# Weight chunks two ahead in the last pair of a part, pinned additions, and another split of the next layer's dots

## The chip, the cores and the metric

The kernel runs on one core of one Trainium2 chip. The metric is the device time of one execution in microseconds; the median of several runs is compared. Five engines work side by side, each through its own instructions in order: TensorE (PE, with its weight loads PEld), VectorE (DVE), ScalarE (ACT), GpSimd (POOL) and SyncE (SP). In this kernel SP only starts transfers from memory; POOL starts those that add into their destination.

## What is computed

Two layers of a decoder trunk on x of 512 tokens by 1024 features. The half of a layer that matters here, cut from the reference:

```
mod = (c_act @ w_ada + b_ada)                      # c_act = silu(c), 1024 numbers
sh1, sc1, g1, sh2, sc2, g2 = jnp.split(mod, 6, axis=-1)
h = rmsnorm(x, norm1_w) * (1 + sc1) + sh1
...                                                # mixers, attention, gates
x = x + g1 * (merged @ w_out)
h2 = rmsnorm(x, norm2_w) * (1 + sc2) + sh2
x = x + g2 * ((jax.nn.silu(h2 @ w_gate) * (h2 @ w_up)) @ w_down)
```

`w_gate` and `w_up` are 1024 x 2816, `w_down` 2816 x 1024: 22 column blocks of 128. The next layer begins with the same norm of the new x, so it needs its own `sc1` and `sh1` by then, and `sc2` and `sh2` later.

## The kernel before

**Layout and numbers.** x lies transposed in on-chip memory, as eight tiles of 128 features by 512 tokens. Every float32 operand of a product is split into a high and a low part (`whi`/`wlo` for weights, two `big` tiles for activations), and a product is three matmuls (`mm3`, L158): high by high, high by low, low by high.

**Weights.** They come in chunks of up to eight 128 x 128 blocks, in the order of use. `next_w(ahead)` (L350) loads until more than `ahead` chunks are waiting (four by default) and hands out the oldest. Loading a chunk means: `fetch` starts its transfer on SP into one of three `raw` buffers, ScalarE copies the high part (`whi`, L326), VectorE subtracts for the low part (`wlo`, L329). There are five `whi` and five `wlo` buffers. The subtraction is pinned: it keeps its place in program order among VectorE's pinned instructions, where a scheduler places the others.

**The feed-forward part.** The 22 column blocks go in four parts, `PARTS` (L47): three blocks along the loop over k, one single and one pair; then three, two and three pairs. After its columns a part runs its down stage: for each of the eight output blocks n it sums over the part's nk = 6, 6, 4, 6 blocks into one PSUM bank, and VectorE adds the result to x (`residual`, L954). A pair (`glu_pair`, L1050) computes two column blocks of gate (z = 0) and up (z = 1) by Strassen-like forms. It uses seven chunks in four steps: B21 and B11; R1 and -V; B22 and T3; T4. TensorE accumulates a[z] over B11, -V, T3 and T4, and VectorE must read a[z] between T3 and T4: `V.tensor_add(m22, m22, a[z])`, L1081, once for each z. The products are then made on ScalarE (`Silu`) and VectorE (L1090, L1092, L1093) and split (`split_from`: high part on ScalarE L511, low part on VectorE L512). A last pair of a part has down chunks behind it; the other pairs have the chunks of the next pair.

**Sums.** Four of the seven chunks of a pair are sums of weight blocks. Per matrix, `Sums.begin` (L250) has POOL load two blocks into `w4` tiles (L255) and add two more on top by transfers (L257); `Sums.first` (L259) lets VectorE add the remaining ones (L263, L264). `w4` has six buffers. `begin` is called four chunks ahead of loading, so the first pair of a part has its sums loaded while the last pair of the part before runs, and the second pair's during the down stage.

**The dots.** `mod` of a layer comes without TensorE: for each of the six vectors and each of eight blocks j, `ada_step` (L397) loads 512 KB of `w_ada` by SP into a `w4` tile and VectorE multiplies it with `csil` and sums along the row (`ada_dot`, L375, one instruction and a short read of the accumulator). `ada_end` (L402) adds the bias and, for SC1 and SC2, folds the norm weight in. `ada_tasks` (L410) makes a list of nine tasks for each vector: eight dots at cost 1.2 and an end at 0.2. Such lists go into a queue `bulk`; each four products of TensorE are a tick, a tick adds `bulk_rate` to a credit, and tasks are issued while the credit isn't negative. The dots of layer 1 for its first norm (SC1, SH1) go to the down stages of parts 0 and 1 of layer 0, those for its second norm to part 2 (five tasks), to the tail of part 3 (four) and to layer 1's loop along k (the rest, at rate 0.6).

**The loop along k.** Layer 1 starts with a loop over the eight k blocks (first three of them in two halves of 256 tokens) that makes q and three feature blocks at once, while VectorE still makes the norm's later k blocks (L482, L485).

Of the kernel before, what the change touches and what calls it, by code (L numbers as in the profile page):

```python
# [46 lines left out]
PARTS = ((3, 1, 1), (0, 0, 3), (0, 0, 2), (0, 0, 3))  # L47

SUMS_AHEAD = 4
AHEAD2 = 5  # L50

RAW, BIG = 3, 46

# [25 lines left out]
def hybrid_trunk(ctx, tc, xT, ws, ada, cols, pool_w, qk_w, crow, pos, con, out):  # L79
# [72 lines left out]
    def pin(ins):  # L152
        return tc.keep_in_program_order(ins)
# [162 lines left out]
                items.append((None, (l, blocks)))  # L316
    at = [0, 0]
    loaded = deque()
    hold = [None]

    def rawt():
        return wp.tile([P, C_BLOCKS, P], F32, tag="raw", name=nm("raw"), bufs=RAW)
# [27 lines left out]
    def next_w(ahead=None):  # L350
        ahead = ahead_now[0] if ahead is None else ahead
        while at[0] < len(items) and len(loaded) <= ahead:
            loaded.append(load_w())
        return loaded.popleft()
# [18 lines left out]
    def ada_dot(aw, l, part, j):  # L373

        return V.scalar_tensor_tensor(aw, aw, 1.0, csil, op0=ALU.mult, op1=ALU.mult,  # L375
                                      accum_out=mod[l][:, part, j:j + 1])
# [20 lines left out]
    def ada_step(l, part, j, early):  # L397
        aw = wp.tile([P, D], F32, tag="raw", name=nm("raw"), bufs=RAW) if early else w4([P, D])
        nc.sync.dma_start(aw, ada[l, part, j])
        pin(ada_dot(aw, l, part, j))  # L400

    def ada_end(l, part):  # L402
        m = mod[l][:, part]
# [6 lines left out]
    def ada_tasks(l, parts, early=False):  # L410
        out = []
        for part in parts:
            for j in range(KT):
                out.append((1.2, lambda part=part, j=j: ada_step(l, part, j, early)))
            out.append((0.2, lambda part=part: ada_end(l, part)))
        return out
# [90 lines left out]
    def split_from(src, scale=None):  # L507

        hi, lo = bigt(), bigt()
        if scale is None:  # L510
            A.activation(hi, src, AF.Copy)  # L511
            V.tensor_sub(lo, src, f32(hi))  # L512
        else:
            A.activation(hi, src, AF.Copy, scale=scale)
            V.scalar_tensor_tensor(lo, src, scale, f32(hi), op0=ALU.mult, op1=ALU.subtract)  # L515
        return hi, lo
# [199 lines left out]
    for l in range(L):  # L716
# [7 lines left out]
        for n, (k, lo, hi) in enumerate([(k, 0, S) for k in range(KT)] if l == 0 else HALVES + REST):  # L724
            if l == 0:
                if k + 3 < KT:
                    first.append(ada_first_load(k + 3))
                if k + 2 < KT:
                    ada_first(k + 2, first[k + 2], SC1)
                    ada_first(k + 2, first[k + 2], SH1)  # L730
                    norm.first_scaled(k + 2)
                    norm.first_hi(k + 2)
                loaded.append(load_w())
                if k + 2 < KT:
                    norm.first_lo(k + 2)
            if k not in held:
                held[k] = next_w(0 if l == 0 else None)
            if l > 0 and n == 1:
                second(norm, l, 0, bank)
                bulk.extend(later)  # L740
                bulk_rate[0] = 0.6
            w = held[k]
            h = norm.k(k)
            for t in range(lo // P, hi // P):
                mm3(q_ps[t], cut(h, slice(None), slice(t * P, (t + 1) * P)), wrow(w, 0), k == 0, k == KT - 1)
            for z in range(3):
                mm3(f_ps[z][:, lo:hi], wblk(w, 4 + z), cut(h, slice(None), slice(lo, hi)),
                    k == 0 and lo == 0, k == KT - 1)
# [298 lines left out]
                mm3(o, wblk(w, 4 * g + c), forms[c][name], start and c == 0, c == HK - 1,  # L1047
                    skip_group_check=not start)

        def glu_pair():  # L1050

            both = range(2)
            e = [ps_pair()[:, 0, :BLOCK] for _ in both]
            a, c = [None] * 2, [None] * 2
            one, two = [None] * 2, [None] * 2
            w = [next_w() for _ in both]
            for z in both:
                group(e[z], w[z], 1, "B21", True)
            for z in both:
                a[z], one[z] = ps_mm()[:, :BLOCK], tmp()  # L1060
                group(a[z], w[z], 0, "B11", True)
                C11 = one[z][:, :BLOCK]
                A.activation(C11, a[z], AF.Copy)
                V.tensor_add(C11, C11, e[z])
            w = [next_w() for _ in both]
            for z in both:
                c[z], two[z] = ps_mm()[:, :BLOCK], tmp()
                group(c[z], w[z], 0, "R1", True)
                A.activation(two[z][:, BLOCK:], c[z], AF.Copy)
            for z in both:  # L1070
                group(a[z], w[z], 1, "-V", False)
                A.activation(one[z][:, BLOCK:], a[z], AF.Copy)
            w = [next_w() for _ in both]
            for z in both:
                group(c[z], w[z], 0, "B22", False)
                C12 = one[z][:, BLOCK:]
                V.tensor_add(C12, C12, c[z])
            for z in both:
                group(a[z], w[z], 1, "T3", False)
                m22 = two[z][:, BLOCK:]  # L1080
                V.tensor_add(m22, m22, a[z])  # L1081
            w = next_w()
            for z in both:
                group(a[z], w, z, "T4", False)

            (g1, u1), (g2, u2) = one, two
            A.activation(g1, g1, AF.Silu)
            A.activation(g2[:, BLOCK:], g2[:, BLOCK:], AF.Silu, scale=-1.0)
            A.activation(g2[:, :BLOCK], a[0], AF.Silu, scale=-1.0)
            V.tensor_mul(u1, u1, g1)  # L1090
            act.append(split_from(u1))
            V.scalar_tensor_tensor(u2[:, BLOCK:], u2[:, BLOCK:], -1.0, g2[:, BLOCK:], op0=ALU.mult, op1=ALU.mult)  # L1092
            V.scalar_tensor_tensor(u2[:, :BLOCK], a[1], -1.0, g2[:, :BLOCK], op0=ALU.mult, op1=ALU.mult)  # L1093
            act.append(split_from(u2))

        for part, (along, single, pairs) in enumerate(PARTS):
            act = []
            nk = along + single + 2 * pairs
            if along:
                held = {}  # L1100
                for n, (k, lo, hi) in enumerate(HALVES + REST):
                    if n == 1:
                        second(norm, l, 1, bank)
                        table(AF.Silu, norm.y[:, 0:1])
                    if k not in held:
                        held[k] = next_w()
                    for z in range(2 * FA):
                        mm3(f_ps[z][:, lo:hi], wblk(held[k], z), cut(norm.k(k), slice(None), slice(lo, hi)),
                            k == 0 and lo == 0, k == KT - 1)
                    if k >= HK:  # L1110
                        make_forms(k - HK)
                del held
                for z in range(FA):
                    glu(f_ps[z], f_ps[FA + z])
            for _ in range(single):
                wg = next_w()
                g = ps_mm()
                feature_tile(g, wg)
                u = ps_mm()
                feature_tile(u, next_w())  # L1120
                glu(g, u)
            bulk_rate[0] = 0.0
            for _ in range(pairs):
                glu_pair()
            if l + 1 < L:
                if part == 0:
                    bulk.extend(ada_tasks(l + 1, (SC1, SH1)))
                    later = ada_tasks(l + 1, (SC2, SH2))
                elif part == 2:
                    bulk.extend(later[:AHEAD2])  # L1130
                    del later[:AHEAD2]
            bulk_rate[0] = 1.5
            blk = Blocks(nk, 4)
            if part + 1 < len(PARTS):
                for n in range(KT):
                    if n == KT // 2:
                        bulk_rate[0] = 0.0
                    o = ps_mm()
                    for k in range(nk):
                        mm3(o, blk(n, k), act[k], k == 0, k == nk - 1)  # L1140
                    residual(n, o, 0, S, G2)
            elif l + 1 == L:
                tail(lambda k: act[k], blk, G2, nk, None, True)
            else:
                flush_bulk()
                drain()
                bulk.extend(later[:4])
                del later[:4]
                bulk_rate[0] = 0.8
                n1 = Norm()  # L1150
                table(AF.Abs_reciprocal_sqrt, f32(act[-1][1])[:, 0:1])
                scratch = ps_pair()
                bank = scratch[:, 1]
                tail(lambda k: act[k], blk, G2, nk, n1, False, lead(n1, l + 1, 0, bank), 4)
                norm = n1
# [100 lines left out]
```

## Time and profile before

| | us |
|---|---|
| median of 3 runs (lowest, highest) | 1468.81 (1468.74, 1469.3) |
| the profiled execution | 1469.42 |
| its span, first to last instruction | 1467.6 |

A profile is of one execution. Its rows give a start and a duration in microseconds from the span's start, the engine, the line, the operation, and output <- inputs with their shape; in brackets stands the engine's idle time ahead of the row and what ended it. `x3` behind a row is a count. A row of the chain of waits gives a start, a length and what the last finisher waited for at that time. `SPq` and the like are an engine's sequencer, and ends of matmuls are modelled. The granted clock of TensorE is full over the whole span.

### The profile page before, as it was taken

How to read it: one execution, taken by the hardware profiler on the slowest of the kernel's cores; microseconds unless marked ns; L12 is line 12 of the kernel's file. 1: busy time of each engine (PE TensorE's matmuls, PEld its weight loads, DVE VectorE, ACT ScalarE, POOL GpSimd, SP SyncE). 2: the span in 40 equal slices, each digit the busy share in tenths (PEclk: the TensorE clock that was granted, in tenths of full speed). 3: DMA queues.
4: the chain of work that ended last, by engine and by line, in shares of the span. 5: the costliest groups of instructions: out<-in, count | busy, mean ns of one | idle time of the engine just before them, and what ended most of it. 6: DMA issues, size and time to landing. Idle time of an engine off the chain costs nothing.

```text
span 1467.6 us, 21944 instructions
## 1 busy us (share of the span) xinstructions
PE 1454.1 (99%) x8443; PEld 1267.3 (86%) x8443; DVE 1055.0 (72%) x1855; ACT 665.3 (45%) x1138; POOL 106.0 (7%) x157
## 2 busy tenths in 40 slices
PE   8999999999999999999999999999999999999999
PEld 6888888788988998989988888778889889989997
DVE  7988888748686876777696867766587757657672
ACT  4634555544453352535444355555335525434450
POOL 0000000001100311221000000000020102111200
PEclk9999999999999999999999999999999999999999
DMA  9635333345337775766434421222462436637431
GB/s 350 224 134 175 127 108 136 130 158 158 101 117 228 201 191 171 205 178 207 161 124 158 160 75 70 74 73 99 158 197 81 133 121 168 188 88 190 134 102 67
DMA packets 84408, 217.18 MB, mean 148 GB/s; under 512 B 10832, under 2 KB 23760, under 8 KB 84304
## 3 DMA queue, kind: packets, MB, share of 16 engines
q1 hardware_dynamic: 67456, 177.37, 35.5%
q0 software_dynamic: 16128, 37.76, 11.7%
q8 instruction: 66, 1.08, 0.3%
q10 hardware_dynamic: 720, 0.66, 0.1%
q14 instruction: 38, 0.31, 0.1%
HBM read 213.65 MB, written 2.10 MB: 147 GB/s over the span
## 4 chain that ended last, share of the span: by engine, by line
PE 89%; DVE 4%; DMA 3%; ACT 2%; issue 1%; SPq 0%; POOL 0%; DVEq 0%; ACTq 0%; POOLq 0%
PE mm L150 76%; PE pair L150 11%; PE mm L156 2%; DMA w<-in_ada 1%; DVE wlo L329 1%; ACT whi L326 1%; DMA w<-in_ws 1%; DVE w L375 1%; DMA raw<-in_ws 1%; DMA x<-in_xT 0%; DVE tmp L1081 0%; DVE big L515 0%; DVE tmp L1090 0%; DVE tmp L482 0%; ACT tmp L613 0%
## 5 line engine op out<-in xcount | busy, mean ns | idle before, releaser
L150 PE MATMUL mm<-big,whi 128*128 128x512 f32 (+1 forms) x4362 | 1082.7, 339 | 5.3 <-DVE tmp L1081 3.6
L150 PEld LDWEIGHTS mm<-big,whi 128*128 128x128 f32 x4362 | 745.4, 190 | 92.8 <-DVE tmp L1081 5.5
L150 PE MATMUL mm<-big,wlo 128*128 128x512 f32 (+1 forms) x2181 | 735.8, 337 | 0.0
L150 PEld LDWEIGHTS mm<-big,wlo 128*128 128x128 f32 x2181 | 413.7, 190 | 44.7
L326 ACT ACTIVATE whi<-raw 128x1024 fp32r<-128x1024 f32 (+2 forms) x240 | 248.8, 1039 | 298.0 <-PE mm L150 261.7
L329 DVE TENSOR_TENSOR wlo<-raw,whi 128x1024 fp32r<-128x1024 f32 (+2 forms) x240 | 284.7, 1193 | 64.7 <-ACT whi L326 64.0
L326 ACT ACTIVATE whi<-w 128x1024 fp32r<-128x1024 f32 x72 | 76.2, 1058 | 147.8 <-PE mm L150 104.3
L954 DVE SCALAR_TENSOR_TENSOR x<-mm,mod,x 128x512 f32<-128x512 f32 (+1 forms) x90 | 61.9, 689 | 93.8 <-PE mm L150 93.7
L255 POOL DMA_DIRECT2D w<-in_ws x72 | 47.6, 670 | 977.6 <-DVE w L375 372.1
L329 DVE TENSOR_TENSOR wlo<-w,whi 128x1024 fp32r<-128x1024 f32 x72 | 86.7, 1221 | 30.7 <-ACT whi L326 30.1
L375 DVE SCALAR_TENSOR_TENSOR w<-w,csil 128x1024 f32<-128x1024 f32 x80 | 95.6, 1220 | 12.1 <-DMA w<-in_ada 11.7
L150 PE MATMUL pair<-whi,big 128*128 128x512 f32 x224 | 76.7, 389 | 0.0
L257 POOL DMA_DIRECT2D w<-in_ws x72 | 64.5, 920 | 146.9 <-DMA w<-in_ws 131.0
L150 PE MATMUL pair<-big,whi 128*128 128x256 f32 (+1 forms) x376 | 74.0, 294 | 0.0
L150 PEld LDWEIGHTS pair<-big,whi 128*128 128x128 f32 x376 | 60.4, 191 | 2.2
L150 PE MATMUL mm<-whi,big 128*128 128x512 f32 x160 | 57.2, 394 | 1.5 <-ACT big L498 1.2
L150 PE MATMUL pair<-big,wlo 128*128 128x256 f32 (+1 forms) x188 | 55.3, 294 | 0.0
L914 DVE SCALAR_TENSOR_TENSOR big<-big,mm 128x512 f32<-128x512 f32 x48 | 32.6, 684 | 26.4 <-PE mm L150 26.1
L512 DVE TENSOR_TENSOR big<-tmp,big 128x512 fp32r<-128x512 f32 x48 | 33.0, 691 | 24.9 <-ACT big L511 24.0
L150 PEld LDWEIGHTS pair<-whi,big 128*128 128x128 f32 x224 | 42.1, 188 | 8.6
L150 PE MATMUL pair<-wlo,big 128*128 128x512 f32 x112 | 43.6, 390 | 0.0
L511 ACT ACTIVATE big<-tmp 128x512 fp32r<-128x512 f32 x48 | 29.6, 620 | 19.7 <-DVE tmp L809 10.6
(187 smaller groups left out, 1241.1 us busy)
## 6 DMA issues: line engine op xcount, KB each, us to landing
raw<-in_ws SPq DMA_DIRECT2D x146, 512.0 KB, 3.3
w<-in_ada SPq DMA_DIRECT2D x80, 512.0 KB, 4.9
w<-in_ws POOLq DMA_DIRECT2D x144, 256.0 KB, 4.7
raw<-in_ws SPq DMA_DIRECT2D x64, 256.0 KB, 4.2
raw<-in_ws SPq DMA_DIRECT2D x24, 384.0 KB, 3.6
raw<-in_ada SPq DMA_DIRECT2D x16, 512.0 KB, 3.3
raw<-in_ws SPq DMA_DIRECT2D x16, 448.0 KB, 5.2
raw<-in_ws SPq DMA_DIRECT2D x36, 128.0 KB, 2.9
```

The costliest lines, as they stand in the source:

```text
L150: tc.keep_in_program_order(T.matmul(*a, **k))
L156: tc.keep_in_program_order(T.transpose(*a))
L255: nc.gpsimd.dma_start(dst, self.source(0, 1))
L257: nc.gpsimd.dma_start(dst, self.source(*other), accum_op=ALU.add)
L326: A.activation(hi[:, :n], raw[:, :n], AF.Copy)
L329: ins = V.tensor_sub(lo[:, :n], raw[:, :n], f32(hi)[:, :n])
L375: return V.scalar_tensor_tensor(aw, aw, 1.0, csil, op0=ALU.mult, op1=ALU.mult, accum_out=mod[l][:, part, j:j + 1])
L511: A.activation(hi, src, AF.Copy)
L512: V.tensor_sub(lo, src, f32(hi))
L914: V.scalar_tensor_tensor(sg, sg, 1.0, branch, op0=ALU.add, op1=ALU.mult)
L954: V.scalar_tensor_tensor(x[k][:, lo:hi], src, mod[l][:, part, k:k + 1], x[k][:, lo:hi], op0=ALU.mult, op1=ALU.add)
```

## The change

Three things. In the last pair of each part, `next_w` gets `ahead = 2` at B22/T3 and at T4, so that fewer down chunks are loaded there and more behind the pair; and the two additions into `m22` are pinned in that pair. The dots of the next layer are spread by `DOTS`: eight tasks in the down stages of parts 0 and 1, two in part 2, none in part 3; five in the tail; the remaining ones, eleven dots, go to the loop along k at rate 0.75 in place of 0.6, and the credit is set to 0 ahead of the tail. And a dot is ordered behind the last split of the part's last pair.

```
-AHEAD2 = 5
+DOTS = (8, 8, 2, 0)
...
-    hold = [None]
+    hold, dots_after, last_split = [None], [None], [None]
...
     def ada_step(l, part, j, early):
         aw = wp.tile([P, D], F32, tag="raw", name=nm("raw"), bufs=RAW) if early else w4([P, D])
         nc.sync.dma_start(aw, ada[l, part, j])
-        pin(ada_dot(aw, l, part, j))
+        with tc.issue_after(dots_after[0].ins) if dots_after[0] is not None else nullcontext():
+            ins = ada_dot(aw, l, part, j)
+        pin(ins)
...
             A.activation(hi, src, AF.Copy)
-            V.tensor_sub(lo, src, f32(hi))
+            last_split[0] = V.tensor_sub(lo, src, f32(hi))
...
                 bulk.extend(later)
-                bulk_rate[0] = 0.6
+                bulk_rate[0] = 0.75
...
-        def glu_pair():
+        def glu_pair(last):
...
-            w = [next_w() for _ in both]
+            w = [next_w(2 if last else None) for _ in both]
             for z in both:
                 group(c[z], w[z], 0, "B22", False)
...
                 group(a[z], w[z], 1, "T3", False)
                 m22 = two[z][:, BLOCK:]
-                V.tensor_add(m22, m22, a[z])
-            w = next_w()
+                ins = V.tensor_add(m22, m22, a[z])
+                if last:
+                    pin(ins)
+            w = next_w(2 if last else None)
             for z in both:
                 group(a[z], w, z, "T4", False)
...
             act.append(split_from(u2))
+            dots_after[0] = last_split[0]
...
-            for _ in range(pairs):
-                glu_pair()
+            for p in range(pairs):
+                glu_pair(p == pairs - 1)
             if l + 1 < L:
                 if part == 0:
-                    bulk.extend(ada_tasks(l + 1, (SC1, SH1)))
-                    later = ada_tasks(l + 1, (SC2, SH2))
-                elif part == 2:
-                    bulk.extend(later[:AHEAD2])
-                    del later[:AHEAD2]
+                    later = ada_tasks(l + 1, (SC1, SH1, SC2, SH2))
+                n = DOTS[part]
+                bulk.extend(later[:n])
+                del later[:n]
             bulk_rate[0] = 1.5
...
                 flush_bulk()
                 drain()
-                bulk.extend(later[:4])
-                del later[:4]
-                bulk_rate[0] = 0.8
+                bulk.extend(later[:5])
+                del later[:5]
+                bulk_rate[0], credit[0] = 0.8, 0.0
```

Seen from the instruction orders of the two programs: TensorE's and POOL's are the same. On SP and VectorE the number of dots in the down stages of parts 0, 1 and 2 of layer 0 goes from 10, 6 and 5 to 8, 7 and 1, that of the tail from 3 to 5 and that of the loop along k from 8 to 11. In each last pair the split of down chunk 1 moves from ahead of the additions to behind the second one into `m22`, and those of chunks 2 and 3 to behind the split of the last product.

## Prediction

> **What bounds the kernel now.** I read the page first: who is busy, and who carries the chain that ended last.
>
> ```profile
> span 1467.6 us, 21944 instructions
> PE 1454.1 (99%) x8443; PEld 1267.3 (86%) x8443; DVE 1055.0 (72%) x1855; ACT 665.3 (45%) x1138; POOL 106.0 (7%) x157
> PE 89%; DVE 4%; DMA 3%; ACT 2%; issue 1%; SPq 0%; POOL 0%; DVEq 0%; ACTq 0%; POOLq 0%
> ```
>
> TensorE has no more than 13.5 us of idle time to give back, and the change leaves its instructions and their order alone. So a gain can only come out of TensorE's waits, and a loss only from a new one. The view of waits for TensorE names the largest:
>
> ```profile
> PE mm L150 <- DVE tmp L1081: 3.6, 9, 1.1
> ```
>
> L1081 is the addition into `m22`, the last read of a[z] before T4 accumulates into it again. There are 18 pairs and only nine waits, so I looked at each in the timeline of TensorE. Three of the nine, each with the matmul ahead of it:
>
> ```profile
> 453.11 0.28 PE L150 MATMUL mm<-big,wlo 128*128 128x256 f32 x1
> 453.65 0.39 PE L150 MATMUL mm<-big,whi 128*128 128x256 f32 x1 [0.26 <-DVE tmp L1081]
> ...
> 505.01 0.28 PE L150 MATMUL mm<-big,wlo 128*128 128x256 f32 x1
> 506.44 0.39 PE L150 MATMUL mm<-big,whi 128*128 128x256 f32 x1 [1.15 <-DVE tmp L1081]
> ...
> 1271.76 0.28 PE L150 MATMUL mm<-big,wlo 128*128 128x256 f32 x1
> 1272.66 0.39 PE L150 MATMUL mm<-big,whi 128*128 128x256 f32 x1 [0.62 <-DVE tmp L1081]
> ```
>
> Matmuls overlap, so a wait's price is the distance of two starts less the usual one. The usual one comes from undisturbed stretches of the chain: 17.33/144 = 0.12 us for 256 columns, and (34.37 - 12 x 0.12)/144 = 0.23 us for 512.
>
> ```profile
> 548.80 34.37 PE mm L150 x156
> ...
> 586.04 17.33 PE mm L150 x144
> ```
>
> The three cost 0.54 - 0.12 = 0.42, 1.31 and 0.78 us: each 0.16 more than the idle time in brackets. All nine cost 3.6 + 9 x 0.16 = 5.0 us. Eight of them stand in the last pair of a part, one in each part of each layer; the one at 506.44 is the first pair of part 1 of layer 0 and has another cause.
>
> **Term 1, the last pairs.** Why the second L1081 is late there shows in VectorE's timeline of the pair at 453:
>
> ```profile
> 450.55 0.42 DVE L1081 TENSOR_TENSOR tmp<-tmp,mm 128x256 f32<-128x256 f32 x1 [0.15 <-PE mm L150]
> 451.09 0.69 DVE L512 TENSOR_TENSOR big<-tmp,big 128x512 fp32r<-128x512 f32 x1
> 452.04 1.23 DVE L329 TENSOR_TENSOR wlo<-raw,whi 128x1024 fp32r<-128x1024 f32 x1 [0.26 <-ACT whi L326]
> 453.18 0.41 DVE L1081 TENSOR_TENSOR tmp<-tmp,mm 128x256 f32<-128x256 f32 x1
> ...
> 456.93 0.69 DVE L512 TENSOR_TENSOR big<-tmp,big 128x512 fp32r<-128x512 f32 x1 [1.04 <-ACT big L511]
> ```
>
> VectorE takes its work in order. A weight split of a later down chunk stands between the two additions and itself waits for ScalarE. The first addition starts right behind T3 of z = 0; T3 of z = 1 is 12 matmuls longer, 1.44 us, so the second could start at 450.55 + 1.44 = 452.0. It starts at 453.18. T4 of z = 1 could begin at 453.11 + 0.12 = 453.2; an addition from 452.0 to 452.4 leaves 0.8 us in hand. In the instruction order of the changed program nothing but the L512 that ends at 451.78 stands between the two, in all eight last pairs; the splits of chunks 2 and 3 come after the split of the last product. So each of the eight waits should go: 5.0 - 1.31 = 3.7 us. Bounds: 0, if the second addition stays late, and 3.8, the eight one by one. The 0.78 at 1272.66 holds 0.35 that the other seven don't, which may belong to that execution; I take 3.6.
>
> Where does the delay go? Chunks 2, 3 and 4 get their splits after the pair, three in a row of 1.22 us, near 457 to 460.5. A down chunk lasts 8 x 3 x 0.23 = 5.5 us, so chunk 2 is wanted 11 us after the pair's end (453.65 + 1.44 - 0.42 = 454.7), near 466: hidden, with 5 us or more. If that cover went, each split would cost up to 1.22 us per part, eight times 2.4 = 20 us; no row hints at it. The two dots behind them start some 2 us later; that is counted below.
>
> **Term 2, parts of two pairs.** With only four k blocks, the down stage reaches the last product early:
>
> ```profile
> 625.96 0.92 PE L150 MATMUL mm<-big,whi 128*128 128x512 f32 x2
> ```
>
> ```profile
> 622.35 3.99 PE mm L150 x22
> 626.34 0.03 issue
> 626.38 19.83 PE mm L150 x86
> ```
>
> The second of the two matmuls from 625.96 on starts at 626.38, so 0.42 - 0.23 = 0.19 us are lost; it is the first that reads the low half of that product. The same code at 455 shows why that half is late: on ScalarE a weight split stands ahead of the product's.
>
> ```profile
> 455.32 1.06 ACT L326 ACTIVATE whi<-raw 128x1024 fp32r<-128x1024 f32 x1 [1.51 <-PE mm L150]
> 456.28 0.61 ACT L511 ACTIVATE big<-tmp 128x512 fp32r<-128x512 f32 x1
> ```
>
> The product was ready when VectorE fell idle, at 456.93 - 1.04 = 455.9. The changed program has the two the other way round, so L511 can start there, 0.4 us earlier. Two such parts: 0 to 0.4 us, I take 0.3.
>
> **Term 3, the wait at 506.** Two views, the chain between 440 and 512 us and POOL's timeline:
>
> ```profile
> 461.07 5.02 DMA w<-in_ada
> ...
> 473.15 4.27 DMA w<-in_ada
> ...
> 490.24 5.73 DMA w<-in_ws
> ...
> 496.26 5.49 DMA w<-in_ws
> ```
>
> ```profile
> 483.62 0.57 POOL L255 DMA_DIRECT2D w<-in_ws  x1 [43.30 <-DVE w L375]
> ```
>
> The dots load into the `w4` buffers that the sums of the coming pairs don't hold; two circulate, so two dots take some 6 us (461.07 to 473.15 is two rounds). Part 0 has ten, and the sums of the second pair get their buffers only from the last two, at 483.6. Their loads then meet the next ones, which take 5.5 to 5.7 us, and VectorE waits for them with the additions behind it:
>
> ```profile
> 501.78 0.69 DVE L263 TENSOR_TENSOR w<-w,raw 128x512 f32<-128x512 f32 x1 [1.45 <-DMA w<-in_ws]
> ```
>
> Part 1 has six dots and no such wait:
>
> ```profile
> 566.30 0.57 POOL L255 DMA_DIRECT2D w<-in_ws  x1 [32.32 <-DVE w L375]
> ...
> 585.39 0.57 POOL L255 DMA_DIRECT2D w<-in_ws  x1 [9.64 <-DVE wlo L329]
> ```
>
> With eight dots the fifth round falls away (-6 us) and the first starts 2 us later: the buffers come free near 479.6, 10 us ahead of the request at 490 instead of 6.6; part 1 has 19. I expect the wait to go: 0 to 1.31 us, I take 1.2.
>
> **Terms against.** Part 1 of layer 0 gets a seventh dot, part 2 one in place of five. The seventh stands ahead of the additions and splits of the coming pair's first weights:
>
> ```profile
> 568.11 1.22 DVE L375 SCALAR_TENSOR_TENSOR w<-w,csil 128x1024 f32<-128x1024 f32 x1
> ...
> 577.04 1.22 DVE L329 TENSOR_TENSOR wlo<-raw,whi 128x1024 fp32r<-128x1024 f32 x1
> ```
>
> ```profile
> 583.16 2.87 PE pair L150 x24
> ```
>
> The sixth dot begins at 568.11; later start (2) and one more load with its dot (4.3 + 1.2) put the seventh's end near 576. Then two additions, at the 0.69 of the row at 501.78, and a split of 1.22 us, all of it twice, bring the second split's end to 581.2; TensorE wants it at 583.16 + 1.44 = 584.6, or 0.4 earlier. 3 us in hand, so 0; bounds 0 and 2.5, should a whole round of 5.5 us have been left out.
>
> The loop along k of layer 1 gets eleven dots instead of seven; in the order of VectorE's instructions, where one more had slipped into it, three are added, in a stretch that has no time left:
>
> ```profile
> 754.00:764.00 10.00, 10.00 (x53) 8.59 (x52) 9.87 (x15) 4.26 (x5) 0.00 (x0) 1.00 0.48 158
> 764.00:774.00 10.00, 10.00 (x45) 8.27 (x45) 8.21 (x13) 2.12 (x2) 0.00 (x0) 1.00 0.62 211
> ```
>
> The columns are the stretch, the busy time of TensorE, its weight loads, VectorE (9.87 and 8.21), ScalarE and POOL, the clock, the DMA share and the rate. Three dots of 1.22 us are 3.7 us. What they push:
>
> ```profile
> 761.88 1.08 DVE L329 TENSOR_TENSOR wlo<-raw,whi 128x896 fp32r<-128x896 f32 x1
> ...
> 772.64 1.23 DVE L329 TENSOR_TENSOR wlo<-raw,whi 128x1024 fp32r<-128x1024 f32 x1 [1.62 <-ACT whi L326]
> ```
>
> ```profile
> 772.37 2.04 PE pair L150 x9
> ```
>
> The first is the split for k = 6, whose matmuls begin 0.7 us ahead of 772.37: nearly 9 us in hand against 3.7. In the changed order six of the eleven loads are issued ahead of the loop, into buffers that earlier dots leave free. Price 0; bounds 0 and the rival below. The Trainium skill, "DMA: Bandwidth & Descriptors", section "Issuing engines are not separate DMA queues", speaks against this edit: every transfer runs on the same 16 engines and interleaves with the others, whoever starts it. By that page's table, at 6.15 us for 1 MB, three more loads of half a MB are, as an estimate, 9 us of transfers; were the weights later by all of that, the 9 us in hand would be used up and the sum be the same. The shares of 0.48 and 0.62 above leave room for it.
>
> **Sum.** 3.6 + 0.3 + 1.2 = 5.1 us. The profiled execution took 1469.42 us, 1.8 more than its span and 0.6 more than the median of the runs; the terms are waits that any execution should have, so I take them off the median: 1468.8 - 5.1 = 1463.7 us.
>
> **Rivals.**
> - The wait at 506 stays: not the dots but the sums' loads themselves are slow. For it: the 5.73 us of the load issued at 490. Against it: POOL's instruction at 483.62 takes 0.57 us as at 585.39, so nothing holds its issue. 1463.7 + 1.2 = 1464.9. The Trainium skill, "SBUF — State Buffer", section "Who interferes with whom", has such a cause: VectorE in some modes locks GpSimd out while it writes descriptors. It excepts two-input additions of the kind that stand here; the equal 0.57 agrees.
> - A new wait for the first weights of a part, behind seven dots or behind the later first dots: 2.5 us, 1466.2.
> - The pins do nothing, because the second addition stays behind the L512 that waits for ScalarE; only the waits at 506 and 626 go: 1468.8 - 1.5 = 1467.3. Against it: that L512 ends 0.3 us before the addition could start.
> - Slower: in the loop along k a dot comes to the head of VectorE before its load has landed, and with it the splits behind. Of the eleven, five aren't issued ahead. If each costs a whole turn of 4.3 + 1.2 us, that is 27.5 us less the 9 in hand, 18.5 late, 1482.2; two turns are 2 us late, 1465.7. It decides for slower from three turns on (16.5 - 9 = 7.5, over 5.1): 1471.2. Against it: in the changed order weight splits stand between these dots, and in the rows of this loop VectorE never waited for a dot's load.
>
> **How the numbers follow.** My forecast 0.6, the wait at 506 stays 0.14, new wait 0.12, pins do nothing 0.08, slower 0.06. The range: the median less every term at its upper bound (5.5), less 0.6 for the scatter of the runs (1468.74 to 1469.3) and 0.4 for bounds read off one execution, gives 1462.3; upward it takes in the first three rivals, 1467.3. The bound of what can be told is 0.2%, 2.9 us: faster below 1465.9. Forecast, first rival and half of the second give faster 0.80; the other half and the third, same 0.14; slower 0.06.
>
> **What would show it.** After: no wait for the `m22` addition in TensorE's view of waits, in any last pair; the two additions 1.5 us apart with one L512 between them; POOL's loads of the sums near 480 and no idle time ahead of the first sum at 502; TensorE without a break at 584 and through the loop along k. Wrong, if a wait for a split (`wlo`) or a sum appears at the start of a pair, or if the second addition still begins a microsecond after T3.

## The result, and the profile after

| | before | after |
|---|---|---|
| median of 6 runs (lowest, highest), us | 1468.92 (1467.93, 1469.95) | 1463.30 (1463.03, 1463.55) |
| span of the profiled execution, us | 1467.6 | 1461.5 |
| ratio, 95% interval | | 0.9955 [0.9944, 0.9966] |

The changed kernel is faster; 1463.7 us was forecast. The page of the profile after, its head, the busy time of the engines and the chain that ended last:

```profile
span 1461.5 us, 21960 instructions
PE 1452.0 (99%) x8443; PEld 1268.2 (87%) x8443; DVE 1053.0 (72%) x1855; ACT 665.8 (46%) x1138; POOL 105.8 (7%) x157
PE 95%; DVE 3%; ACT 1%; DMA 1%; issue 0%; SPq 0%
```

TensorE now carries 95% of the chain instead of 89%, VectorE 3 instead of 4, transfers 1 instead of 3. TensorE's view of waits begins like this (what it waited for, us in total, times, longest):

```profile
PE mm L151 <- ACT big L501: 1.2, 1, 1.2
PE pair L151 <- POOL ones L199: 1.1, 1, 1.1
PE mm L151 <- ACT big L912: 1.0, 2, 0.5
PE mm L151 <- DVE big L488: 0.9, 4, 0.3
```

The addition into `m22`, which is L1085 in the changed file, has no row any more, in place of 3.6 us in nine waits. VectorE's timeline at the last pair of part 0, and TensorE's at the place where it had stood still from 453.11 to 453.65:

```profile
450.69 0.42 DVE L1085 TENSOR_TENSOR tmp<-tmp,mm 128x256 f32<-128x256 f32 x1 [0.15 <-PE mm L151]
451.23 0.69 DVE L515 TENSOR_TENSOR big<-tmp,big 128x512 fp32r<-128x512 f32 x1
452.13 0.42 DVE L1085 TENSOR_TENSOR tmp<-tmp,mm 128x256 f32<-128x256 f32 x1 [0.20 <-PE mm L151]
452.47 1.22 DVE L330 TENSOR_TENSOR wlo<-raw,whi 128x1024 fp32r<-128x1024 f32 x1
```

```profile
453.25 0.28 PE L151 MATMUL mm<-big,wlo 128*128 128x256 f32 x1
453.37 0.40 PE L151 MATMUL mm<-big,whi 128*128 128x256 f32 x2
```

The second addition starts 1.44 us behind the first, at once when T3 of z = 1 is done, with one L515 (L512 before) between the two; the weight split comes behind it. TensorE goes on in its usual step of 0.12 us. I compared the starts of equal matmuls in the two traces (the two have 8443, in one order) and noted where the lead of the changed kernel grows: by 0.50 to 0.58 us at seven of the last pairs and by 0.86 at the one at 1272, 4.6 us together; by 0.29 and 0.30 in the two parts of two pairs; by 1.41 at the first pair of part 1, where the wait at 506 had been. That is 6.6 us, less 0.1 lost earlier: 6.5 at the last matmul, 6.1 in the spans, 5.6 in the medians. No place has a new loss.

### The profile page after: what moved, and what is told of

It reads as the page before. It is cut to its first block, busy times and chain, and to the rows that moved or that the text cites. A ratio compares the mean times of both kernels' runs of the same rounds, so it can differ in the third digit from the quotient of the medians.

```text
span 1461.5 us, 21960 instructions
## 1 busy us (share of the span) xinstructions
PE 1452.0 (99%) x8443; PEld 1268.2 (87%) x8443; DVE 1053.0 (72%) x1855; ACT 665.8 (46%) x1138; POOL 105.8 (7%) x157
## 4 chain that ended last, share of the span: by engine, by line
PE 95%; DVE 3%; ACT 1%; DMA 1%; issue 0%; SPq 0%
PE mm L151 81%; PE pair L151 12%; PE mm L157 2%; DVE wlo L330 1%; ACT whi L327 0%; DMA w<-in_ada 0%; DMA x<-in_xT 0%; DVE w L376 0%; ACT tmp L616 0%; ACT tmp L618 0%; DVE tmp L485 0%; DVE big L504 0%; DVE big L518 0%; DVE big L488 0%; DVE w L635 0%
## 5 line engine op out<-in xcount | busy, mean ns | idle before, releaser
L515 DVE TENSOR_TENSOR big<-tmp,big 128x512 fp32r<-128x512 f32 x48 | 33.0, 691 | 22.4 <-ACT big L514 21.6
```

The costliest lines, as they stand in the source:

```text
L515: last_split[0] = V.tensor_sub(lo, src, f32(hi))
```

## The experiments

Each was run beside the kernel before, on one chip within a group. The kernel before scatters more on those chips than in the runs above (1467.8 to 1476.4 us over all groups), so ratios are given, and the waits are read in the traces.

**The pairs alone.** The kernel before, with the change in `glu_pair` only:

```
-            w = [next_w() for _ in both]
+            w = [next_w(2 if last else None) for _ in both]
...
-                V.tensor_add(m22, m22, a[z])
-            w = next_w()
+                ins = V.tensor_add(m22, m22, a[z])
+                if last:
+                    pin(ins)
+            w = next_w(2 if last else None)
```

> The kernel before with the change of the last pairs alone (weights two chunks ahead, the additions pinned); the dots stay as they were, ten in part 0 of layer 0. Theory (the terms are separate): the eight waits of the last pairs and the two short breaks after them go, the wait near 501 (506 in the kernel before) stays at about 1 us. By the traces' leads the eight were worth 4.6 and the two breaks 0.6, so 5.2 in the trace, and about 4.5 in the medians: 1464.4 us. Rival A (the wait at 506 goes with the pairs, not with the dots): no wait for the second addition is left and the time is that of the changed kernel, 1463.3. Rival B (most of the gain comes from the dots): 1467 or more.

Measured: 1471.03 us against 1470.74, ratio 1.000 [0.999, 1.0011]. This is neither the theory nor rival A, and rival B only in its time: by the medians all of the gain is given back, with 1.5 us either way left open by the interval. In the trace the eight waits and the two short breaks do go (lead by lead as in the changed kernel, 5.2 us), but two larger waits stand in their place and take back 3.9 us against the kernel before. TensorE's view of waits, and VectorE's timeline at the two places:

```profile
PE mm L150 <- DVE tmp L1081: 4.8, 2, 2.8
```

```profile
503.01 0.69 DVE L263 TENSOR_TENSOR w<-w,raw 128x512 f32<-128x512 f32 x1 [2.35 <-DMA w<-in_ws]
...
661.42 0.69 DVE L263 TENSOR_TENSOR w<-w,raw 128x512 f32<-128x512 f32 x1 [3.08 <-DMA w<-in_ws]
```

The first is the wait of the kernel before, grown from 1.45 us of idle VectorE to 2.35. The second, in the first pair of part 3, is new. Both wait for a sum's transfer. The chain of waits between 440 and 512 us shows how such a transfer got late: the dots behind the pair begin later, the `w4` buffers go to the sums later, and the sums' transfers then run beside one another and beside those of the next weights.

```profile
479.69 1.23 DVE w L375 x2
...
486.99 2.93 DMA w<-in_ws
...
491.51 5.18 DMA w<-in_ws
...
496.98 6.00 DMA w<-in_ws
```

A transfer of 256 KB takes 2.93 us at first, then 5.18 and 6.00; the last of the three adds into its destination. The Trainium skill, "DMA: Bandwidth & Descriptors", section "Anatomy of one DMA — SWDGE (gpsimd) path", gives 2.0 us and one us for each 436 KB for a transfer of this path, 2.6 us for 256 KB as an estimate: the first comes near it, the others took twice that or more. (This execution had lost about 0.9 us by 30 us, where the granted clock from 18 to 24 us is 0.72; the first place that the edit moves lies near 450 us. The last section comes back to the clock.)

**The dots alone.** The changed kernel with `glu_pair` as it was before (the diff above, backwards).

> The changed kernel with the pairs as they were before; the new places of the dots alone. Theory: only the wait at 506 goes; eight waits of the last pairs remain, 3.5 us or so in the view of waits. 1.2 to 1.4 us are gained: 1467.4 (1467.1 to 1467.8). Rival (the dots' places also cost or bring something elsewhere, in part 1's first weights or in the loop along k, and the pairs hide it): above 1468.5 or below 1466.5.

Measured: 1468.18 us, ratio 0.9987 [0.9978, 0.9996], so 1.9 us (0.6 to 3.2). The theory holds for the waits: the trace has none near 506, and of the `m22` addition's waits exactly those of the last pairs are left. They are shorter than the 3.5 us expected, since 3.6 less the 1.1 at 506 is 2.5, and the wait at 1272 is no longer than the others here. The median lies 0.4 us above the expected range.

```profile
PE mm L151 <- DVE tmp L1085: 2.1, 8, 0.3
```

So by the ratios the parts are worth 0 and 1.9 us each by itself and 6.6 (5.0 to 8.2) together; by the medians 0, 2.6 and 5.6. They are not separate.

**Ten and nine dots in part 0.** `DOTS = (12, 4, 2, 0)` and `DOTS = (10, 6, 2, 0)`, tasks with the one that ends a vector, in place of `(8, 8, 2, 0)`; part 0 then has ten and nine dots, part 1 five and six.

> The same with ten dots in part 0, as before the change, and five in part 1. Theory: the wait comes back whole, an idle time of VectorE near 1.4 us ahead of a sum and a TensorE wait near 1.1 for the m22 addition of part 1's first pair: 1464.6. Rival: no wait, 1463.3.

> The changed kernel with nine dots in part 0 of layer 0 and six in part 1 (instead of eight and seven). Theory (the wait near 501 comes from the dots' loads running into the sums' loads): a half step. One dot more takes about 3 us; buffers come free near 482.5 instead of 479.7, and the sum's load that lands near 501 is 0 to 0.7 us late: a wait of 0 to 0.7, 1463.3 to 1464. Rival (the wait was an accident of how transfers met, not of the dots' number): no trend over eight, nine and ten, any of 1463.3 to 1465.

Measured: 1466.67 us for ten, ratio 0.9972 [0.9959, 0.9985], and 1463.74 for nine, 0.9954 [0.994, 0.9967], the changed kernel's own ratio. With ten the wait is back and a second one is new, for a split at the start of the pair; with nine there is neither. The waits of the run with ten:

```profile
PE mm L151 <- DVE tmp L1085: 1.8, 1, 1.8
...
PE pair L151 <- DVE wlo L330: 0.7, 1, 0.7
```

The theory holds in kind: by the medians the ninth dot costs 0.4 us and the tenth 2.9. It fails in size, since 1464.6 was expected for ten. One reason shows in the granted clock, the column ahead of the DMA share in the rows by stretches (columns as in the prediction):

```profile
506.00:509.20 3.20, 1.36 (x11) 1.16 (x11) 2.84 (x6) 2.51 (x4) 0.87 (x1) 1.00 1.08 301
509.20:512.70 3.50, 3.50 (x19) 3.50 (x19) 2.74 (x5) 1.23 (x3) 1.13 (x2) 0.51 0.85 222
```

TensorE stood still for 1.84 us until 508.43. From 509.2 on it runs at half its clock for 3.4 us, and by the starts of equal matmuls it falls another 1.4 us behind the changed kernel there, beyond the 2.1 us of the wait itself.

**Five dots in part 2.** `DOTS = (8, 8, 6, 0)`: part 2 gets five dots as before the change, the tail four and the loop along k eight (the expectation said seven).

> The changed kernel with five dots in part 2 of layer 0 (as before the change) instead of one, and accordingly seven instead of eleven in the loop along k of layer 1; parts 0 and 1 keep eight and seven. In the run with the pairs changed alone, TensorE waited 2.8 us near 663, in the first pair of part 3, where the kernel before has no wait. Theory (the last pair's new order starts the dots later, and five dots in part 2 then hand their buffers to the sums too late): the wait near 660 comes back at 2 to 3 us, none near 501; 1465.5 to 1466.5 us. Rival (that wait was the backlog of the late part 0, or chance in the transfers): no wait, 1463.3.

Measured: 1466.44 us, ratio 0.998 [0.997, 0.9989]. The wait is there, at 661.51 in this trace and alone:

```profile
PE mm L151 <- DVE tmp L1085: 1.4, 1, 1.4
```

It is smaller in the profiled execution (the fastest of ten, 1465.23) than in the run with the pairs alone; the median lies where the theory put it. So the dots that the change takes out of part 2 pay for the later start that the last pair brings.

**Ten dots in part 1.** `DOTS = (8, 12, 0, 0)` and rate 2.0 in part 1.

> The changed kernel with ten dots in part 1 of layer 0 instead of seven (and none in part 2, nine instead of eleven in the loop along k). The prediction left 3 us in hand behind the seventh; in the changed trace the second split of the next pair's first weights ends at 578.2 and is wanted near 581.9. There a dot took 2.75 us, so three more are 8.3 us, 4.6 beyond the hand. Theory: one new wait for a split (wlo) or a sum at the start of part 2, 3 to 6 us: 1466.3 to 1469.3. Rival (the first weights pass the dots, or the loads run faster when nothing else is wanted): no wait, 1463.3.

Measured: 1466.24 us, ratio 0.9972 [0.9962, 0.9982]. There is no wait for a split at the start of part 2. A sum is late there by 0.85 us of idle VectorE, and TensorE waits for the `m22` addition behind it, 0.6 us in the profiled execution, which is the fastest of the nine (1463.39):

```profile
PE mm L151 <- DVE tmp L1085: 0.6, 1, 0.6
```

So in this trace the three dots cost time through the same buffers as in part 0, not by standing ahead of the first weights. It holds only 0.8 us of loss against the changed kernel's trace; where the other executions, 2.9 us above the changed kernel by the median, lost theirs is not shown.

These runs share one measure. For each start of a part, the time from POOL's first load of a sum for the second pair to the first matmul of the part's first pair, and VectorE's idle time ahead of that sum (all from the timelines):

| part | kernel | load, us | pair, us | ahead, us | idle, us |
|---|---|---|---|---|---|
| 1 | after | 479.70 | 487.48 | 7.8 | 0 |
| 1 | nine dots | 482.30 | 488.76 | 6.5 | 0 |
| 1 | before | 483.62 | 487.86 | 4.2 | 1.45 |
| 1 | pairs alone | 485.18 | 488.19 | 3.0 | 2.35 |
| 1 | ten dots | 486.37 | 488.19 | 1.8 | 2.15 |
| 2 | after | 569.89 | 580.72 | 10.8 | 0 |
| 2 | ten dots in part 1 | 576.79 | 580.44 | 3.7 | 0.85 |
| 3 | after | 629.88 | 642.87 | 13.0 | 0 |
| 3 | before | 638.46 | 646.04 | 7.6 | 0 |
| 3 | pairs alone | 640.28 | 645.88 | 5.6 | 3.08 |
| 3 | five dots in part 2 | 637.16 | 642.72 | 5.6 | 1.66 |

In these traces, one execution each, there is no wait from 6.5 us on, and always one at 5.6 and below. (In part 3, with five dots in part 2, the view names no releaser for POOL's load, but in all three kernels it starts 0.56 us after the fourth dot's accumulator is read.) Two dots more (eight to ten) take 6.0 us of it, the new last pair takes 1.2 us (part 1) and 2.0 (part 3). The kernel before stood at 7.6 in part 3, just on the right side.

**No order for the dots.** The changed kernel without `dots_after[0] = last_split[0]`:

> The changed kernel without the order that holds the dots behind the split of the last product. In VectorE's order three dots of part 1 of layer 0 now stand ahead of the last pair's C12 and m22 additions and one behind them, ahead of three weight splits; nothing else moves. Theory: a dot whose load has not landed holds VectorE with the additions behind it, and TensorE waits for the additions: one or two new waits of 2 to 6 us together, 1465.3 to 1469.3. Rival (the loads are in place by then, or the stretch has VectorE time to spare): 1463.3, as the changed kernel.

Measured: 1465.93 us, ratio 0.9968 [0.9957, 0.9978]. Waits of TensorE, and VectorE's timeline in the last pair of part 1:

```profile
PE mm L151 <- DVE tmp L1085: 1.8, 1, 1.8
```

```profile
541.78 1.23 DVE L376 SCALAR_TENSOR_TENSOR w<-w,csil 128x1024 f32<-128x1024 f32 x1 [3.69 <-DMA w<-in_ada]
```

The theory holds: VectorE stood 3.69 us at a dot whose load had not landed, and the additions behind it came late. Again the clock falls to half, right behind TensorE's wait, which ended at 547.39:

```profile
547.40:551.00 3.60, 3.60 (x17) 3.60 (x18) 2.50 (x4) 2.86 (x5) 0.00 (x0) 0.53 0.79 294
```

Against the changed kernel's trace the wait costs 2.1 us and this stretch another 1.5. The dot at VectorE's head is what the slower rival feared for the loop along k, in another place.

**Sixteen dots in the loop along k.** The tail's `bulk.extend(later[:5])` taken out and `bulk_rate[0] = 1.1` in the loop:

> The changed kernel with the five dots of the last down stage moved into the loop along k of layer 1: sixteen there instead of eleven. By the prediction 9 us were in hand and three dots took 3.7; 5.3 are left, and five more dots are 6.1 us on VectorE and 2.5 MB more of loads. Theory: just used up, 0 to 2.5 us in one wait for a weight split (wlo): 1463.3 to 1465.8. Rival (a dot comes to VectorE's head before its load has landed, a turn of 5.5 us each for those not issued ahead): 7 us or more, above 1470. Rival (the hand is larger than read): 1463.3.

Measured: 1463.30 us, ratio 0.9957 [0.9942, 0.9972], the changed kernel's time. The rows by stretches (columns as in the prediction) of the sixteen, then of the changed kernel:

```profile
760.00:770.00 10.00, 10.00 (x45) 8.27 (x45) 9.96 (x18) 1.06 (x1) 0.00 (x0) 1.00 0.99 395
770.00:780.00 10.00, 10.00 (x46) 8.27 (x45) 10.00 (x18) 8.41 (x14) 0.31 (x1) 1.00 0.82 303
```

```profile
754.00:764.00 10.00, 10.00 (x46) 8.27 (x45) 9.93 (x17) 1.64 (x2) 0.00 (x0) 1.00 0.70 234
764.00:774.00 10.00, 10.00 (x46) 8.29 (x45) 7.33 (x12) 3.50 (x4) 0.00 (x0) 1.00 0.81 292
```

VectorE has no time left at all, the DMA engines are at a share of 0.99, and TensorE is at 10.00 all the same. The hand was larger than read. The splits that TensorE wants next keep their places between the dots: the one for k = 6 in the changed kernel, with the pair that its matmuls run into (timeline of VectorE, chain of waits):

```profile
758.59 1.09 DVE L330 TENSOR_TENSOR wlo<-raw,whi 128x896 fp32r<-128x896 f32 x1
```

```profile
768.69 2.04 PE pair L151 x9
```

It ends at 759.7 and is wanted at 768.0, 8.3 us in hand where the kernel before had 8.7. With sixteen dots the same split starts at 757.88 and TensorE reaches its pair at 768.37, with 8.7 us. The Trainium skill, "DMA: Bandwidth & Descriptors", section "Issuing engines are not separate DMA queues", which the prediction set against this edit, speaks of shared engines; here they are shared up to 0.99 and nothing that TensorE waits for is late.

**Work put between the two additions.** The changed kernel with one operation of 512 or 1024 columns, or two of 1024, behind the first `m22` addition of each last pair; it takes the maximum of `csil` with itself, which leaves `csil` as it is:

```
                 if last:
                     pin(ins)
+                    if z == 0:
+                        pin(V.scalar_tensor_tensor(csil[:, :512], csil[:, :512], 1.0, csil[:, :512], op0=ALU.mult, op1=ALU.max))
```

> The changed kernel with one extra VectorE operation of 512 columns (some 0.7 us) between the two m22 additions of every last pair. The prediction gave the second addition 0.8 us in hand. In the changed trace the first addition starts at 450.69, so with the extra operation and the L515 the second would start near 452.5, against 452.13 without it; TensorE wants it to start by 452.9. Theory (only lateness beyond that hand costs): no wait for L1085, time of the changed kernel, 1463.3 within 0.5. Rival (VectorE's work in this stretch costs time in itself): eight times 0.7, 1468.9.

> The same with one operation of 1024 columns (pitch 1.14 us): second addition from about 452.9, just at the limit. Theory: waits of 0 to 0.1 us in the view of waits, with the restart of TensorE's stream 0 to 0.35 us each, 0 to 2.8 together: 1464.3. Rival as above: eight times 1.14, 1472.4.

> The same with two operations of 1024 columns: second addition from about 454.0, 1.1 us beyond the limit. Theory: eight waits of 1.1 us less the 0.1 of the usual gap in the view of waits, and with the 0.16 and 0.10 that a restart adds 1.35 each: 10.8 together, 1474 (1472.5 to 1475.5). Rival (the wait in the kernel before came from the split's own wait for ScalarE, not from the time on VectorE): under 1466.

Measured, one execution each: 1464.06, 1463.69 and 1472.28 us. The first two have no wait for L1085. The first lies 0.8 us above the changed kernel's median, more than the 0.5 allowed for, but in its trace the last pairs lead the kernel before by the same amounts as the changed kernel's do. In the second, L515 went behind both additions, so the second addition was no later (452.08, 1.47 us behind the first): that run doesn't test the limit. The third does. VectorE's and TensorE's timelines:

```profile
450.40 0.42 DVE L1085 TENSOR_TENSOR tmp<-tmp,mm 128x256 f32<-128x256 f32 x1 [0.15 <-PE mm L151]
450.74 1.22 DVE L1090 SCALAR_TENSOR_TENSOR csil<-csil 128x1024 f32<-128x1024 f32 x1
451.87 0.68 DVE L515 TENSOR_TENSOR big<-tmp,big 128x512 fp32r<-128x512 f32 x1
452.48 1.22 DVE L1090 SCALAR_TENSOR_TENSOR csil<-csil 128x1024 f32<-128x1024 f32 x1
453.61 0.41 DVE L1085 TENSOR_TENSOR tmp<-tmp,mm 128x256 f32<-128x256 f32 x1
```

```profile
452.96 0.28 PE L151 MATMUL mm<-big,wlo 128*128 128x256 f32 x1
454.08 0.50 PE L151 MATMUL mm<-big,whi 128*128 128x256 f32 x2 [0.84 <-DVE tmp L1085]
454.42 0.28 PE L151 MATMUL mm<-big,wlo 128*128 128x256 f32 x1
```

The matmul starts 0.47 us behind the addition that it waits for. Without the extra work it would have started at 452.96 + 0.12 = 453.08, so the addition could start at 452.61; T3 lets it start at 450.40 + 1.44 = 451.84. That is 0.8 us in hand, as the prediction had it. Eight waits cost 8.2 to 8.6 us against the two shorter runs, less than the 10.8 expected: a wait delays its matmul by 1.00 us and the next by 0.10, and I had added the restart's 0.16 to a limit that holds it already, with 0.1 too much lateness. Occupied VectorE time beyond the hand is what costs, with nothing waiting for ScalarE.

**Which half of the edit acts.** This needs no run: without the two pins the changed kernel is the same program, instruction for instruction and wait for wait, and with the pins but without `next_w(2)` it is the same as with neither. So the run of the dots alone is also the run without `next_w(2)`. The pins are idle; loading two chunks ahead does it.

**A version on top.** The waits that head the list now, at the start of the gate and up stage (L487, L488), come from the normalisation of the first blocks. With three instead of two column blocks halved at the end of the output projection:

```
-        tail(lambda k: merged[k], Blocks(KT), G1, KT, n2, False, lead(n2, l, 1, bank))
+        tail(lambda k: merged[k], Blocks(KT, 3), G1, KT, n2, False, lead(n2, l, 1, bank), 3)
```

> The changed kernel with three instead of two column blocks halved at the end of the output projection, for the waits at the start of the gate and up stage that the change leaves alone (three breaks in each layer, for the scaling and the addition of the first normalised blocks: 0.36, 0.53 and 0.35 us by the distances of starts in the changed kernel's trace). Theory: the residual and the statistics of the first half come earlier against the matmuls that want them, the breaks go; 2.5 us less about 0.6 for the 256-column matmuls in place of 512-column ones: 1461.4. Rival (the breaks are set by the chain of the normalisation, which starts no earlier): 1463.3 to 1464.

Measured: 1461.32 us (1461.21 to 1462.39, 5 runs), ratio 0.9941 [0.9929, 0.9954], as the theory has it. The rows for L487 and L488 are gone from TensorE's waits. It ran beside the kernel before and not beside the changed kernel; its slowest run is 0.6 us below the fastest of that.

## Why the prediction was right, point by point

**Term 1** (3.6 us) had the right mechanism. The second addition starts when T3 is done, the split is behind it, none of the eight waits is left, and the 0.8 us in hand is confirmed by the extra work. The size was short: the leads say 4.6. Of these, 0.35 is the extra at 1272.66. It is gone as well in the run of the dots alone, which leaves the pairs as they were, so it belonged to that execution, as the prediction suspected. The eight waits themselves are worth 4.2 us, and 3.4 by the prediction's price of 0.42 each (it took 3.6). I had priced a wait at the distance of the two starts around it. The matmul behind those is late too, before the change

```profile
453.65 0.51 PE L150 MATMUL mm<-big,whi 128*128 128x256 f32 x2 [0.26 <-DVE tmp L1081]
453.99 0.29 PE L150 MATMUL mm<-big,wlo 128*128 128x256 f32 x1
```

and with the extra work above (454.08 to 454.42): two starts take 0.34 us where 0.24 is usual. That is 0.1 us more for each wait.

**Term 2** (0.3) is 0.6 by the leads, above its bound of 0.4, for the same reason: behind the 0.19 us of each break the next matmul came 0.34 us later instead of 0.23.

**Term 3** (1.2) is 1.4 for the wait at 506, and its working holds: POOL's first load moved to 479.70 where "near 479.6" was forecast, and two dots move that load by 5.5 to 6.7 us (485.18 with the pairs alone and 486.37 with ten dots, against 479.70), where some 6 was forecast. The wait's rival, slow loads whatever the dots do, falls with the run of ten dots, which has the wait, and that of nine, which hasn't.

What the sum did not see is that the terms hang together. The prediction counted the dots' later start only where it worked on part 0 and part 1. The same 2 us also reach part 3, where 7.6 us ahead become 5.6. Left alone, the first edit gained nothing by the medians; the sum was right because the second edit takes four dots out of part 2 and two out of part 0. By its own split the pairs are worth 3.9 us and the dots 1.2; measured by the ratios, the pairs are worth 0 by themselves and 6.6 - 1.9 = 4.7 once the dots have moved, the dots 1.9 by themselves and 6.6 once the pairs have changed. The medians would put the 4.7 at 5.6 - 2.6 = 3.0. The traces, place by place, say 4.2 + 0.6 = 4.8: the eight waits and the two short breaks are what the run of the dots alone still has and the changed kernel has not.

That the time came within 0.4 us of the forecast is in part luck. The terms were 1.5 us short by the leads (5.1 against 6.6), and the medians of the two kernels lie 0.9 us closer together than the last matmuls of their traces (5.6 against 6.5).

**Terms against.** Seven dots in part 1 cost nothing. Timeline of VectorE after, the seventh dot and the second split of the next pair, and the chain:

```profile
570.85 1.22 DVE L376 SCALAR_TENSOR_TENSOR w<-w,csil 128x1024 f32<-128x1024 f32 x1 [1.53 <-DMA w<-in_ada]
...
576.99 1.22 DVE L330 TENSOR_TENSOR wlo<-raw,whi 128x1024 fp32r<-128x1024 f32 x1
```

```profile
580.88 2.87 PE pair L151 x24
583.75 16.25 PE mm L151 x135
```

The split ends at 578.2 and is wanted at 580.88 + 1.44 = 582.3: 4.1 us in hand, 3 forecast. (By the prediction's own rows the seventh dot ends at 568.11 + 1.22 + 2 + 5.5 = 576.8 and not near 576, which leaves 2; it came at 572.1.) But the limit that bites first is another, as the run with ten dots there shows: the buffers of the sums, 10.8 us ahead by the table's measure, where the kernel before had 583.00 - 566.30 = 16.7. The eleven dots of the loop cost nothing, and sixteen wouldn't either; of the 3.7 us that I let them take from the 9 in hand, 0.4 were taken (8.7 before, 8.3 after).

**The rivals.** No wait at 506 stayed, none was new, and the slower one did not show in the loop. The rival that the pins do nothing is right in its words and wrong in its time: the pins are idle, but the chunks two ahead put the split behind the addition without them.

## What to carry to other kernels

A buffer pool that two kinds of work share makes their edits one edit: measure each alone as well, since one may gain nothing until the other makes room. Read how long ahead of its use a shared buffer's refill is issued, in every part and not only in the one that waits now; here, in one trace each, 6.5 us were enough and 5.6 were not. An instruction in an in-order queue that stands ahead of an urgent one costs only what goes beyond the urgent one's time in hand, so a full engine need not be late.

## What the runs showed of the hardware

A stall of TensorE's stream of 256-column matmuls costs about 0.26 us beyond the idle time that the profile shows: 0.16 at the waiting matmul, 0.10 at the next; the wait of 2.77 us with the pairs alone cost 3.03.

A longer stall can cost more. Over all fourteen traces, their first 7 and last 4 us left out, TensorE waits eight times for 1.84 us or more. Behind five of these waits, 0.1 to 1.7 us after their end, the granted clock is one half for 3.41 us: near 20 us with the pairs alone, the dots alone and nine dots, at 509 with ten dots and at 547 without the order. In the last two this stretch cost 1.4 and 1.5 us. Behind the other three (1.97, 2.05 and 2.77 us) the clock stayed full, and so it did behind every wait of 1.51 us or less. That the wait brings the lower clock about is the plain reading; no run varied the wait's length to test it, and what decides between the five and the three is open.

The kernels with a late sum scatter: the ten runs with ten dots in part 0 lie between 1465.4 and 1468.6 us, the ten with five in part 2 between 1465.2 and 1468.3, while the changed kernel's six lie within 0.5 us and the four with sixteen dots in the loop within 1.2. With five dots in part 2 the four longest times (1467.2 and more) are the four with a mean granted clock below 1.000, so the clock may be part of it. It is not all a matter of late sums, though: nine dots in part 0, with none in the trace, scatter from 1462.7 to 1467.3. Each kernel has one trace, so which waits differ from one execution to the next is not shown.
